# Opening stage of a hybrid diffusion layer on channel-major inputs: token sums by matmul, scalings moved from GpSimd to other engines, late modulation sums formed as columns

## The chip, the cores and the metric

The kernel runs on one core of one Trainium2 chip. Its engines are TensorE (PE in the profile, with its weight loads as PEld), VectorE (DVE), ScalarE (ACT), GpSimd (POOL) and SyncE (SP), whose queue starts all the loads that matter here. The metric is the device time of one execution in microseconds (us). The kernel before took 1308.92 us, the median of 3 runs (1308.15 to 1310.53).

## The reference, cut to what matters

The reference is one layer of a diffusion backbone: 512 latent tokens `x` and 256 context tokens `ctx`, each of 1024 channels, attention and a gated DeltaNet side by side, then a gated MLP. The change touches its first lines, where shift and scale vectors are made from a condition `c`, and both token streams are normalised and modulated with them:

```python
def rms_norm(x, gain=None):
    y = x32 * lax.rsqrt(jnp.mean(x32 * x32, axis=-1, keepdims=True) + NORM_EPS)
...
mod_lat = jax.nn.silu(c) @ w_mod + b_mod          # 6 vectors of 1024: sh1 sc1 g1 sh2 sc2 g2
mod_ctx = jax.nn.silu(c_ctx) @ w_mod + b_mod
hx = modulate(rms_norm(x), sh1, sc1)              # h * (1 + scale) + shift
hc = modulate(rms_norm(ctx), csh1, csc1)
ak_x, av_x, qkv_x, ... = split_cols(hx @ w_in)    # everything else needs hx and hc
```

The first two vectors (`sh1`, `sc1`) are needed at once, by both streams. The other four are needed for the latent stream alone, and late.

## The kernel before

**Precision.** Most products are made from pairs: a 32-bit operand is split into a rounded "hi" (written by ACT as a copy in the type fp32r) and the rest "lo" (a DVE subtraction), and three matmuls (hi·hi, hi·lo, lo·hi) take the place of one. The helper `split` (line 122) does this, `mm3` (126) issues the three matmuls. A matmul on plain 32-bit operands shows up in the profile as two records.

**Opening stage (lines 414 to 583).** Tokens come in with the token on the partition: `xs0` holds the context, `xs1` and `xs2` the latents, 1 MB each. ACT squares each 128x1024 piece and sums it along the row (line 461), GpSimd takes the power -1/2 (`rsqrt`, 172 to 175), and DVE scales the piece in place (465). `x_cols` (502) then turns the scaled tokens channel-major with TensorE transposes, 48 in all, and copies them from PSUM into `stash`, by DVE and ACT in turn.

In the meantime the first 2048 columns of `w_mod` come in as 8 tiles `wm` of 1 MB, in a ring of 3. `gemv(nb)` (469), four of them, multiplies two such tiles by the two condition vectors: the first `FKS[nb]` of the 8 contraction steps as split pairs `wmh`/`wml` (`FKS = '4466'`), the others as plain 32-bit matmuls. `GN = '023'` puts half of the `wml` subtractions of blocks 0, 2 and 3 on GpSimd. `mod_cols(nb)` (489) turns the result into columns of `mod` and `modc`, through a DVE copy `mrow`, 4 small transposes and 4 small DVE additions. Each block `nb` frees two of the 8 channel tiles: `modulate(kp)` (514) scales and shifts those two, for the latents with DVE, for the context with GpSimd (`YV = 2`), and splits the results `hf` into `hxH`/`hxL` and `hcH`/`hcL`. `early_proj(k)` (533) then does the part of channel tile `k` of the first two projections of `w_cm`: 12 matmuls, of 256 and of 512 columns, half each.

**What sets the order.** Between `pinned[0] = True` (541) and 576 every matmul keeps its place in the program, and that place is written out by hand in the string `ORD` (39): `d` is a run of filler matmuls on zeros, `x` is `x_cols`, `g` `gemv`, `m` `mod_cols`, `y` `modulate`, `p` `early_proj`. The loads keep the order of `LORD` (56). Other instructions of DVE, ACT and GpSimd are ordered by a planner, which uses costs of its own and two priorities here: `sooner` (x, g, m, d) goes ahead of `first` (y). Each engine then runs its own list strictly in order.

**The stage behind it (lines 698 to 757).** It begins with the first matmul into `pq` and makes keys, values and queries for six blocks of `w_aq`. Into it `late_mods` (362) is woven, step by step: it computes the other 4096 columns of the modulation (8 groups `q` of 512). ACT, DVE and GpSimd sum 8 scaled tiles `wmd` of the weights into `macc`, 128 partitions by 512. `total(q)` sums over the partitions by a plain matmul with a column of ones as the stationary side (128x1) and `macc` as the moving side (512 columns), giving a row; ACT copies the row to SBUF. `columns(q)`, three steps later, turns the row into 4 columns by 4 transposes, and DVE adds the bias. Both take their PSUM tile from `xbank` (186), which has one buffer (`NX = 1`). What follows (attention, DeltaNet, MLP) is not touched by the change.

Of the kernel before, what the change touches and what calls it, by code (L numbers as in the profile page):

```python
# [6 lines left out]
F32 = mybir.dt.float32  # L7
# [7 lines left out]
P = 128  # L15
# [33 lines left out]
MV, MT, CT = 0, 6, 9  # L49
# [6 lines left out]
LORD = 'x0 x1 x2 w0 w1 w2 w3 h0 h1 w4 w5 w6 w7'  # L56
WB = 3
# [21 lines left out]
def hybrid_layer_body(tc, x, ctxt, xT, consts, cols, rows, w_mod1, w_mod2, w_db, w_aq, w_cm, w_pa, w_pd, w_out,  # L79
# [54 lines left out]
    with es:  # L134
# [227 lines left out]
        def late_mods():  # L362
# [28 lines left out]
            for i in range(9 * KT + CT - 7):  # L391
                for at, fn in ((MT, total), (CT, columns)):
                    q = (i - KT - at) // KT
                    if (i - at) % KT == 0 and 0 <= q < 8:
                        fn(q)
                if i < 8 * KT:
                    part(i // KT, i % KT)
                yield
# [16 lines left out]
        with m1_es:  # L415
            m1 = m1_es.enter_context(tc.tile_pool(name="m1", bufs=1))
            mps = m1_es.enter_context(tc.tile_pool(name="mps", bufs=NB, space=PSUM))
            xs = [m1.tile([P, 2, D], F32, name=f"xs{i}") for i in range(3)]
            wms = []

            def ordered_load(out, in_):
                i = SP.dma_start(out, in_)
                if LPIN:
                    tc.keep_in_program_order(i)

            hw = []
            for op in LORD.split():
                i = int(op[1])
                with sooner():
                    if op[0] == "w":  # L430
                        wms.append(m1.tile([P, 4, 512], F32, name="wm", tag="wm", bufs=WB))
                        ordered_load(wms[i], w_mod1[i // 2, i % 2])
                    elif op[0] == "h":
                        h, part = order[i]
                        raw = ws.tile([P, 1024], F32, name="wraw", tag="wraw", bufs=2)
                        ordered_load(raw, w_cm[8 * part + h])
                    elif i == 0:
                        ordered_load(xs[0], ctxt)
                    else:
                        ordered_load(xs[i], x[:, 2 * i - 2:2 * i, :])  # L440
# [16 lines left out]
            ss = m1.tile([P, 6], F32, name="ss")  # L457
            rs = m1.tile([P, 6], F32, name="rs")
            for i in range(3):
                for t in range(2):  # L460
                    act(hxH[:, 6:8, :].rearrange("p a b -> p (a b)"), xs[i][:, t, :], AF.Square, accum_out=ss[:, 2 * i + t:2 * i + t + 1])
                sl = slice(2 * i, 2 * i + 2)
                rsqrt(rs[:, sl], ss[:, sl], 1.0 / D, EPS)
                for t in range(2):
                    ts(xs[i][:, t, :], xs[i][:, t, :], rs[:, 2 * i + t:2 * i + t + 1], ALU.mult)
            m2 = lambda t, o: t[:, o:o + 16].rearrange("p (s k) -> p s k", s=2)
            wsl = lambda k: slice(k * P, k * P + P)

            def gemv(nb, k0=0, k1=KT):
# [3 lines left out]
                for k in range(k0, k1):  # L473
                    wm, j = wms[2 * nb + k // 4], k % 2
                    if k >= int(FKS[nb]):
                        mm(ps[0:2], cs[:, 2 * k:2 * k + 2], wm[:, k % 4, :], False, k == KT - 1)
                        continue
                    if j == 0:
                        wmh = m1.tile([P, 2, 512], F32R, name="wmh", tag="wmh", bufs=WHB)
                        wml = m1.tile([P, 2, 512], F32R, name="wml", tag="wml", bufs=WHB)  # L480
                        act(wmh, wm[:, k % 4:k % 4 + 2, :])
                        tt(wml, wm[:, k % 4:k % 4 + 2, :], wmh, ALU.subtract, G if k % 4 == 0 and str(nb) in GN else V)
# [16 lines left out]
            sides = ((hxH, hxL, mod, hx_pair), (hcH, hcL, modc, hc_pair))  # L499
            stash = [[pair(F32) for _ in range(KT // 2)] for pair in (hx_pair, hc_pair)]  # L500

            def x_cols(j):
                i, kp = j // 4, j % 4
                dst = stash[1][kp] if i == 0 else stash[0][kp][:, :, 256 * i - 256:256 * i]
                pt = mps.tile([P, 2, 256], F32, name="pt", tag="pt", bufs=NB - PMB - NS)
                for a in range(2):
                    for t in range(2):
                        transpose(pt[:, a, t * P:(t + 1) * P], xs[i][:, t, wsl(2 * kp + a)])
                if j % 2 or j < XV:
                    act(dst, pt)  # L510
                else:
                    V.tensor_copy(dst, pt)

            def modulate(kp):
                for (hh, hl, md, pair), st in zip(sides, stash):
                    n = hh.shape[2]
                    hfs = []
                    for a in range(2):
                        k = 2 * kp + a
                        hf = m1.tile([P, n], F32, name="hf", tag="hf%d" % n, bufs=HB)  # L520
                        if n == NL or YV:
                            ts(hf, st[kp][:, a, :], md[:, 8 + k:9 + k], ALU.mult, md[:, k:k + 1], ALU.add,
                               G if YV == 2 and n < NL else V)
                        else:
                            act(hf, st[kp][:, a, :], AF.Identity, scale=md[:, 8 + k:9 + k], bias=md[:, k:k + 1])
# [20 lines left out]
            def warm(n):  # L546
                pz = mps.tile([P, 512], F32, name="pt", tag="pt", bufs=NB - PMB - NS)
                for i in range(4 * n):
                    mm(pz, wz[:, 0:P], wz)


            def step(what, i):
                if what == "g":
                    with sooner():
                        gemv(i)
                elif what in "ab":
                    with sooner():
                        gemv(i, 0 if what == "a" else 4, 4 if what == "a" else KT)
                elif what == "m":
                    with sooner():  # L560
                        mod_cols(i, mrows[i])
                elif what == "d":
                    with sooner():
                        warm(i)
                elif what == "x":
                    with sooner():
                        x_cols(i)
                elif what == "y":
                    with first():
                        modulate(i)  # L570
                else:
                    early_proj(i)

            for op in ORD.split():
                step(op[0], int(op[1:]))
# [936 lines left out]
def _layout(i):  # L1512
# [5 lines left out]
    a["x"] = f(x.reshape(4, P, D).transpose(1, 0, 2))  # L1518
    a["ctxt"] = f(cx.reshape(2, P, D).transpose(1, 0, 2))
    a["xT"] = f(x.T.reshape(KT, P, NL).transpose(1, 0, 2))  # L1520
# [41 lines left out]
_ORDER = ["x", "ctxt", "xT", "consts", "cols", "rows", "w_mod1", "w_mod2", "w_db", "w_aq", "w_cm", "w_pa", "w_pd",  # L1562
# [21 lines left out]
```

## Time and profile before

| | us |
|---|---|
| median of 3 runs (lowest, highest) | 1308.92 (1308.15, 1310.53) |
| profiled execution, its own time | 1304.85 |
| span of its instructions | 1303.1 |
| opening stage: from the span's start to the first matmul into `pq` | 70.49 |
| stage behind it: to the first matmul of attention scores (`pS`) | 184.48 |
| busy over the span: PE, DVE, ACT, POOL | 1224.8, 846.9, 625.9, 308.9 |

How to read it: the span runs from the first to the last instruction of one profiled execution, and 1.75 us of that execution's time lie around it. An engine counts as busy from the start to the end of each instruction, and matmuls overlap, so a busy PE can still be one that could go faster. A line number such as L108 is that of the helper which issues the instruction (`tt` is 107 to 108, `ts` 110 to 114, `act` 119 to 120, `mm` 131 to 132 with its matmul recorded at L87), so groups are told apart by the names of their tiles: out<-in.

### The profile page before, as it was taken

Reading aid. Unit: us, or ns where it says so; the run is one execution under the profiler, and the core shown is the slowest. Engines: PE = TensorE matmul, PEld = TensorE weight load, DVE = VectorE, ACT = ScalarE, POOL = GpSimd, SP = SyncE. Lnnn points to the kernel's source line nnn. Section 1 sums busy time; section 2 is a strip of 40 time slices with the busy share of each in tenths; the row PEclk is TensorE's granted clock in tenths of the full one; section 3 lists DMA queues with packets and bytes.
Section 4 is the critical chain, followed back from the end, with each engine's and each line's share of the span. In section 5 each row is a group of like instructions: output and inputs, shape, how many; then the busy total and the mean of one; then the engine's idle time right before and its main releaser. Section 6 shows DMA issues by size and latency. Waiting matters only on the chain.

```text
span 1303.1 us, 20844 instructions
## 1 busy us (share of the span) xinstructions
PE 1224.8 (94%) x7835; PEld 1024.0 (79%) x7835; DVE 846.9 (65%) x1625; ACT 625.9 (48%) x1403; POOL 308.9 (24%) x364
## 2 busy tenths in 40 slices
PE   6899999999967999899998999999999999999997
PEld 3487878899856878778787888778988888888886
DVE  5886977777759986675665556555676666653223
ACT  5454656666576665474444443233454444442221
POOL 1753420000133249659546400000000000000000
PEclk9999999999989999999999999999999999999998
DMA  8656731121383342543632654374032323332331
GB/s 318 228 169 200 233 109 65 65 82 57 116 239 104 123 141 93 177 135 106 195 123 97 188 169 147 120 234 155 19 112 97 97 97 97 97 93 89 98 93 66
DMA packets 70790, 170.82 MB, mean 131 GB/s; under 512 B 7872, under 2 KB 18720, under 8 KB 69280
## 3 DMA queue, kind: packets, MB, share of 16 engines
q1 hardware_dynamic: 70688, 169.47, 39.4%
q8 instruction: 62, 1.02, 0.3%
q14 instruction: 40, 0.33, 0.1%
HBM read 144.23 MB, written 25.21 MB: 130 GB/s over the span
## 4 chain that ended last, share of the span: by engine, by line
PE 66%; POOL 11%; DVE 8%; DMA 5%; issue 3%; ACT 3%; SPq 0%; POOLq 0%; DVEq 0%; ACTq 0%
PE mc L87 32%; PE mb L87 17%; POOL R L108 4%; PE pq L87 4%; POOL prod L108 4%; PE pb L87 4%; PE pS L87 3%; PE ab L87 2%; PE ab L91 1%; DMA Gb<-gamdr 1%; DMA M<-gamdr 1%; PE xb L91 1%; DVE wlo L108 1%; PE pk L87 1%; DMA sz<-gdr 1%
## 5 line engine op out<-in xcount | busy, mean ns | idle before, releaser
L108 DVE TENSOR_TENSOR wlo<-wraw,whi 128x1024 fp32r<-128x1024 f32 x152 | 187.5, 1235 | 163.3 <-ACT whi L120 161.1
L120 ACT ACTIVATE whi<-wraw 128x1024 fp32r<-128x1024 f32 x152 | 159.0, 1048 | 207.3 <-PE mc L87 112.0
L87 PE MATMUL mb<-hxH,whi 128*128 128x512 f32 x384 | 163.6, 426 | 3.2 <-DVE R L108 3.0
L87 PE MATMUL mb<-hxL,whi 128*128 128x512 f32 x384 | 153.6, 400 | 0.0
L87 PE MATMUL mb<-hxH,wlo 128*128 128x512 f32 x384 | 153.2, 399 | 0.0
L87 PE MATMUL mc<-h2H,whi 128*128 128x512 f32 (+1 forms) x376 | 142.9, 380 | 0.3 <-ACT whi L120 0.3
L87 PE MATMUL mc<-h2H,wlo 128*128 128x512 f32 (+1 forms) x376 | 142.1, 378 | 0.5 <-DVE wlo L108 0.5
L87 PE MATMUL mc<-h2L,whi 128*128 128x512 f32 (+1 forms) x376 | 140.7, 374 | 0.0
L108 POOL TENSOR_TENSOR rc<-rc,mhalf 128x2 f32<-128x2 f32 x4 | 3.2, 812 | 461.2 <-DVE rc L114 461.2
L87 PEld LDWEIGHTS mb<-hxH,wlo 128*128 128x128 f32 x384 | 73.1, 190 | 18.0
L87 PEld LDWEIGHTS mb<-hxH,whi 128*128 128x128 f32 x384 | 73.9, 192 | 14.8 <-issue 3.2
L87 PEld LDWEIGHTS mc<-h2H,wlo 128*128 128x128 f32 x376 | 70.5, 188 | 15.3 <-DVE wlo L108 1.0
L87 PEld LDWEIGHTS mb<-hxL,whi 128*128 128x128 f32 x384 | 73.7, 192 | 10.1
L87 PEld LDWEIGHTS mc<-h2L,whi 128*128 128x128 f32 x376 | 70.6, 188 | 13.7
L87 PEld LDWEIGHTS mc<-h2H,whi 128*128 128x128 f32 x376 | 70.7, 188 | 12.7 <-ACT whi L120 0.5
L87 PE MATMUL mc<-aH,whi 128*128 128x512 f32 (+1 forms) x198 | 73.4, 371 | 0.6 <-DVE x L117 0.6
L87 PE MATMUL mc<-aH,wlo 128*128 128x512 f32 (+1 forms) x198 | 73.1, 369 | 0.0
L87 PE MATMUL mc<-aL,whi 128*128 128x512 f32 (+1 forms) x198 | 73.1, 369 | 0.0
L117 DVE SCALAR_TENSOR_TENSOR u<-mc,col,u 128x511 f32<-128x511 f32 x88 | 65.4, 747 | 1.4
L108 POOL TENSOR_TENSOR prod<-X,R 128x31 f32<-128x31 f32 (+15 forms) x93 | 53.5, 575 | 22.2 <-DVE X L108 15.3
L108 POOL TENSOR_TENSOR R<-R,prod 128x31 f32<-128x31 f32 (+15 forms) x93 | 57.1, 614 | 6.8
L87 PE MATMUL pq<-whi,hxH 128*128 128x256 f32 x192 | 55.8, 291 | 0.0
(354 smaller groups left out, 3069.8 us busy)
## 6 DMA issues: line engine op xcount, KB each, us to landing
wraw<-in_w_cm_dram SPq DMA_DIRECT2D x48, 512.0 KB, 3.9
wraw<-in_w_up_dram SPq DMA_DIRECT2D x44, 512.0 KB, 3.7
wmd<-in_w_mod_dram SPq DMA_DIRECT2D x64, 256.0 KB, 3.7
wm<-in_w_mod_dram SPq DMA_DIRECT2D x8, 1024.0 KB, 8.9
wraw<-in_w_down_dram SPq DMA_DIRECT2D x16, 512.0 KB, 3.6
wraw<-in_w_aq_dram SPq DMA_DIRECT2D x12, 512.0 KB, 4.9
M<-gamdr SPq DMA_DIRECT2D x64, 64.0 KB, 4.5
wraw<-in_w_pa_dram SPq DMA_DIRECT2D x8, 512.0 KB, 4.0
```

What stands on the lines that cost most here:

```text
L87: i = nc.tensor.matmul(*a, **k)
L91: i = nc.tensor.transpose(*a, **k)
L108: (eng or V).tensor_tensor(out=out, in0=a, in1=b, op=op)
L117: V.scalar_tensor_tensor(out=out, in0=a, scalar=s, in1=b, op0=op0, op1=op1)
L120: A.activation(out, a, f, **kw)
```

## The change

- `x` and `ctx` are loaded channel-major (`xT` as 4 loads of 512 KB into `stash`, `ctxT` as one of 1 MB into `cin`). The 48 transposes, the copies out of PSUM and the scaling of `xs` go.
- `sums(i)`, for i = 0 to 5, takes 128x1024 elements: ACT squares them into `sq` (a ring of 2), DVE adds the two halves, and 4 plain 32-bit matmuls with the squares as the stationary side (128x128) and a 128x128 block of ones as the moving side add up over channels, so that each token's sum stands on its partition. After the last one two DVE operations and one GpSimd power give `rc`, 128x6.
- `spread()` makes diagonal blocks from `rc` (DVE) and multiplies them by ones (plain 32-bit matmuls of 512 and 256 columns), which gives the factor of each token on every partition, in PSUM. `normal(kp)`, four of them, multiplies `stash` by it on DVE.
- The `hf` of `modulate` are made by ACT for both streams. All `wml` are made by DVE (`GN = ''`). `FKS` goes from 4466 to 2466.
- `wm` comes in as 16 tiles of 512 KB in a ring of 7.
- `ORD` changes: 12 filler matmuls in place of 16; `gemv` 0 in two halves (`a0`, `b0`) around `spread`; `p0` and `p1` together behind `m1`; `p2` and `p3` behind `m2`; `p4` to `p7` behind `m3`. `HB`, the ring of `hf`, goes from 2 to 3. `r` and `s` have the priority `sooner`, `n` has `first`.
- In `late_mods` `total` goes; `columns(q)` stands where `total(q)` stood, and makes the 4 columns directly, by 4 plain matmuls with a 128x128 block of `macc` as the stationary side and one column of ones as the moving side.

```diff
-GN = '023'
-FKS = '4466'
-ORD = 'd4 x0 x1 x2 x3 x4 x5 x6 x7 g0 x8 x9 x10 x11 m0 y0 g1 m1 y1 p0 g2 p1 m2 y2 p2 g3 p3 m3 p4 y3 p5 p6 p7'
+GN = ''
+FKS = '2466'
+ORD = 'd3 s0 s1 s2 s3 s4 s5 a0 r0 n0 n1 n2 n3 b0 m0 y0 g1 m1 y1 p0 p1 g2 m2 y2 p2 p3 g3 m3 y3 p4 p5 p6 p7'
-HB = 2
+HB = 3
-LORD = 'x0 x1 x2 w0 w1 w2 w3 h0 h1 w4 w5 w6 w7'
-WB = 3
+LORD = 'c0 x0 x1 x2 x3 w0 w1 w2 w3 h0 h1 w4 w5 w6 w7'
+WB = 7
...
-            def total(q):
-                ps = xbank()[0:1, :, :].rearrange("p a b -> p (a b)")
-                mm(ps, ones[:, 0:1], accs[q][1])
-                act(accs[q][0][0:1, :], ps)
-
             def columns(q):
                 pst = xbank()[:, 0, 0:4]
                 for i in range(4):
-                    T.transpose(pst[:, i:i + 1], accs[q][0][0:1, i * P:(i + 1) * P], ident[0:1, 0:1])
+                    mm(pst[:, i:i + 1], accs[q][1][:, i * P:(i + 1) * P], ones[:, 0:1])
                 tt(mod[:, 16 + 4 * q:20 + 4 * q], pst, col[:, S_BMOD + 16 + 4 * q:S_BMOD + 20 + 4 * q], ALU.add)
...
+            def sums(i):
+                n = (NCX, NL)[i > 1]
+                src = cin[:, 4 * i:4 * i + 4, :] if i < 2 else stash[0][i - 2]
+                sq = m1.tile([P, 1024 // n, n], F32, name="sq", tag="sq", bufs=2)
+                act(sq, src, AF.Square)
+                h = 512 // n
+                tt(sq[:, 0:h], sq[:, 0:h], sq[:, h:2 * h], ALU.add)
...
+                for a in range(h):
+                    for t in range(n // P):
+                        mm(pv[-1][:, t, :], sq[:, a, wsl(t)], ones, i in (0, 2) and a == t == 0,
+                           i in (1, 5) and a == h - 1 and t == n // P - 1)
+                if i == 5:
+                    for o, t in ((4, pv[0][:, 0:2, 0]), (0, pv[1][:, :, 0])):
+                        sl = slice(o, o + t.shape[1])
+                        ts(rc[:, sl], t, 1.0 / D, ALU.mult, EPS, ALU.add)
+                    tt(rc, rc, mhalf[:, 0:6], ALU.pow, G)
+
+            def spread():
+                for s in range(2):
...
+                    tt(dg, ident.unsqueeze(1).to_broadcast([P, n, P]),
+                       rc[:, 4 * s:4 * s + n].unsqueeze(2).to_broadcast([P, n, P]), ALU.mult)
+                    mm(pr[:, 0:n * P], ones, flat(dg))
+                    prs.append(pr[:, 0:n * P])
+
+            def normal(kp):
+                for s in range(2):
+                    tt(stash[s][kp], stash[s][kp], prs[s].unsqueeze(1).to_broadcast([P, 2, prs[s].shape[1]]), ALU.mult)
...
-                        tt(wml, wm[:, k % 4:k % 4 + 2, :], wmh, ALU.subtract, G if k % 4 == 0 and str(nb) in GN else V)
+                        tt(wml, wm, wmh, ALU.subtract, G if k % 4 == 0 and str(nb) in GN else V)
...
-                        if n == NL or YV:
-                            ts(hf, st[kp][:, a, :], md[:, 8 + k:9 + k], ALU.mult, md[:, k:k + 1], ALU.add,
-                               G if YV == 2 and n < NL else V)
-                        else:
-                            act(hf, st[kp][:, a, :], AF.Identity, scale=md[:, 8 + k:9 + k], bias=md[:, k:k + 1])
+                        act(hf, st[kp][:, a, :], AF.Identity, scale=md[:, 8 + k:9 + k], bias=md[:, k:k + 1])
```

More of the change, by code (lines that the diff above doesn't have):

```diff
@@ L48 @@
 NS = 2
-MV, MT, CT = 0, 6, 9
+MV, MT = 0, 6
 MACT, MK, MU = 1, 2.6, 0
@@ L417, in hybrid_layer_body @@
             mps = m1_es.enter_context(tc.tile_pool(name="mps", bufs=NB, space=PSUM))
-            xs = [m1.tile([P, 2, D], F32, name=f"xs{i}") for i in range(3)]
-            wms = []
+            sides = ((hxH, hxL, mod, hx_pair), (hcH, hcL, modc, hc_pair))
+            cin = m1.tile([P, KT, NCX], F32, name="cin")
+            stash = [[hx_pair(F32) for _ in range(KT // 2)], [cin[:, 2 * i:2 * i + 2, :] for i in range(KT // 2)]]
+            wms, hw = [], []
             def ordered_load(out, in_):
[L422 to L426, printed above, removed]
+                tc.keep_in_program_order(SP.dma_start(out, in_))
             for op in LORD.split():
```

97 lines of the change are left out of this document (34 added, 63 removed).

## The prediction

> **What bounds the kernel now.** I first read busy time by stage: the opening from 29.4 to 70.5 us in two stretches, then the stage behind it in two.
>
> ```profile
> core 0: us, PE busy (x) PEld busy (x) DVE busy (x) ACT busy (x) POOL busy (x), PEclk, DMA share, GB/s
> 29.40:49.40 20.00, 16.99 (x67) 7.28 (x65) 17.14 (x28) 11.44 (x17) 13.57 (x7) 0.91 0.87 325
> 49.40:70.50 21.10, 18.65 (x96) 12.55 (x96) 16.32 (x26) 7.76 (x14) 16.04 (x10) 1.00 0.34 113
> 70.50:130.00 59.50, 56.17 (x428) 49.08 (x427) 45.57 (x109) 29.09 (x78) 21.70 (x18) 1.00 0.61 197
> 130.00:184.50 54.50, 51.91 (x401) 45.40 (x400) 52.44 (x151) 33.13 (x102) 23.43 (x16) 1.00 0.61 198
> ```
>
> In the opening no engine is full: DVE has 17.14 of 20.00 us, and GpSimd carries 13.57 and 16.04. Behind it PE is nearly full, and in the second half DVE too. Next, the waits up to 70.5 us, and every instruction on the tiles `wml` and `hf` (shortest/median/longest in ns).
>
> ```profile
> POOL hf L114 <- DVE modc L108: 13.5, 3, 11.6
> ACT hxH L120 <- DVE hf L114: 11.0, 4, 4.3
> ```
> ```profile
> L108 POOL TENSOR_TENSOR wml<-wm,wmh x5: 2391/2476/3367, 17.8 to 51.5; 128x1024 fp32r<-128x1024 f32 x5
> L108 DVE TENSOR_TENSOR wml<-wm,wmh x5: 1209/1214/2630, 20.7 to 50.0; 128x1024 fp32r<-128x1024 f32 x5
> ```
> ```profile
> L114 DVE TENSOR_SCALAR hf<-hxL,mod x8: 534/544/2214, 30.0 to 61.8; 128x512 f32<-128x512 f32 x8
> L120 ACT ACTIVATE hxH<-hf x8: 612/626/635, 30.7 to 62.5; 128x512 fp32r<-128x512 f32 x8
> L114 POOL TENSOR_SCALAR hf<-hcL,modc x8: 553/1566/3114, 31.8 to 64.2; 128x256 f32<-128x256 f32 x8
> L108 DVE TENSOR_TENSOR hxL<-hf,hxH x8: 677/682/721, 33.2 to 63.2; 128x512 fp32r<-128x512 f32 x8
> L120 ACT ACTIVATE hcH<-hf x8: 417/418/421, 35.0 to 64.7; 128x256 fp32r<-128x256 f32 x8
> L108 DVE TENSOR_TENSOR hcL<-hf,hcH x8: 424/426/1507, 35.5 to 66.2; 128x256 fp32r<-128x256 f32 x8
> ```
>
> GpSimd needs 2.48 us for a subtraction that takes DVE 1.21, and DVE's own runs stretch up to 2.63 us (an `hf` from 0.54 to 2.21). So the modulation, GpSimd and ACT waiting for DVE in turn, limits the opening more than the matmuls do.
>
> **The opening, part by part.** I follow PE, whose order is written out, and let the other engines hold it up. The rows for its pace:
>
> ```profile
> 94.73 3.00 PE pq L87 x24
> 97.73 8.30 PE mb L87 x48
> 108.87 0.95 PE xb L87 x2
> 112.86 0.34 PE xb L91 x4
> ```
> ```profile
> 22.80 3.60 PE L87 MATMUL pm<-wm,cs 128*2 128x512 f32 x8
> ```
> ```profile
> 917.97 0.60 PE L87 MATMUL mc<-dg,cst 128*128 128x128 f32 x4
> ```
> ```profile
> 6.85 1.06 ACT L120 ACTIVATE hxH<-xs 128x1024 fp32r<-128x1024 f32 x1 [2.25 <-DMA xs<-in_ctxt_dram]
> ```
>
> 24 matmuls of 256 columns take 3.00 us, 0.125 each. The 8.30 us hold 24 of 256 and 24 of 512, which leaves 0.22 for one of 512. A plain 32-bit one of 512 columns (two records) costs 3.60/4 = 0.90, one of 128 columns 0.60/2 = 0.30. One `early_proj` is 6 x 0.125 + 6 x 0.22 = 2.1.
>
> Sums: the context lands at 6.85 as now. Square 1.06, addition 0.68 (the `hxL` row, same shape), 4 matmuls 1.2: 2.94 us per piece, and with two buffers one piece each 1.5. PE starts at 8.6 and ends at 8.6 + 5 x 1.5 + 1.2 = 17.3, if its clock is full. It may not be:
>
> ```profile
> 8.00:9.00 1.00, 0.00 (x0) 0.00 (x0) 0.00 (x0) 0.97 (x3) 0.00 (x0) 1.00 1.03 434
> 12.00:13.00 1.00, 1.00 (x6) 1.00 (x5) 0.39 (x1) 0.00 (x0) 0.70 (x1) 0.50 1.02 434
> 15.00:16.00 1.00, 0.75 (x5) 0.42 (x4) 0.23 (x1) 0.97 (x3) 0.00 (x0) 1.00 0.99 418
> ```
>
> After some idle microseconds the granted clock was 0.50 at 12, and 1.00 again at 15. The change leaves PE idle for some 3 us ahead of the first sums, so I charge one piece's matmuls twice: +1.2, end at 18.5. The Trainium skill ("TensorE: Matmul & The Clock Gate", "What's actually happening") has the clock halved after an idle window of about 3.4 us and restored after a busy one, which speaks against fewer fillers; by a full window the end would be about an estimated 19.0. The same page ("PE-mode transpose") says that transposes don't count as busy work for this; the trace disagrees, as only transposes ran between 11 and 15, so swapping them for matmuls buys no clock.
>
> Then `a0`: 2 split steps (4 x 0.22) and 2 plain (1.8), 2.7, to 21.2. This hides the reciprocals: the power, two small DVE operations and the diagonals (0.68 + 0.43, as additions of 512 and 256), some 2 us that would all show without `a0`.
>
> ```profile
> 9.46 0.70 POOL L108 TENSOR_TENSOR rs<-rs,mhalf 128x2 f32<-128x2 f32 x1 [9.02 <-DVE rs L114]
> ```
>
>  `spread` 0.9 + 0.45, to 22.5; `b0` 4 x 0.9, to 26.1. For the turn into columns:
>
> ```profile
> L487 DVE COPY mrow<-pm 4x512 f32<-4x512 f32 x4 | 2.7, 674 | 1.6 <-PE pm L87 1.6
> L120 ACT ACTIVATE t<-pc,col 128x256 f32<-128x256 f32 x2 | 0.9, 472 | 3.8 <-PE pc L87 3.8
> L120 ACT ACTIVATE t<-mb,col 128x512 f32<-128x512 f32 x1 | 0.7, 690 | 0.2 <-PE mb L87 0.2
> L108 DVE TENSOR_TENSOR mod<-xb,mod 128x4 f32<-128x4 f32 x4 | 0.7, 163 | 0.1
> ```
>
> `m0`: copy 0.67, transposes 0.34, some 0.4 of hops: 1.4, to 27.5. Now block 1 starts at 29.46:
>
> ```profile
> 29.46 0.39 PE L87 MATMUL pm<-wmh,cs 128*4 128x512 f32 x1
> 70.49 0.28 PE L87 MATMUL pq<-whi,hcH 128*128 128x256 f32 x1
> ```
>
> so some 2 us are won by here. `FKS` costs PE 1.8 - 0.9 = 0.9 in it and saves DVE a `wml`. `g1` (8 x 0.22 + 3.6) and `m1` run to 34.3.
>
> Is `p0` ready by then? DVE is free for this from about 18.9, and must do: 3 `wml` and 2 `wlo` (5 x 1.21), diagonals 1.1, `normal` 4 x (1.21 + 0.68) = 7.6, two `mrow` 1.3, four `mod` additions 0.6, `y0` 2 x 0.68 + 2 x 0.43 = 2.2, together 18.9. Back to back these overlap a little (I take off 6%, as 1.14 against 1.21 in this row), so 17.8, to 36.7.
>
> ```profile
> 91.55 1.14 DVE wlo L108
> ```
>
> DVE is late by 2.4 us, because `normal` is new and all `wml` now lie there. From 36.7: `p0` `p1` 4.2, `g2` 12 x 0.22 + 1.8 = 4.5, `m2` 1.4, `p2` `p3` 4.2, `g3` 4.5, `m3` 1.4, `p4` `p5` 4.2, to 61.1. `y3` starts behind `m3` at 56.9 with 0.6 of additions, then ACT: 2 x 0.69 + 2 x 0.63 + 2 x 0.47 + 2 x 0.42 = 4.4, then an `hcL` 0.43, to 62.4. `p6` and `p7` end at 66.6, against 70.49: -3.9. The ends: with PE alone in charge (2.4 less) and no cold sums (1.2 less) 63.0, -7.5; with more gaps on DVE 71.2, +0.7, below.
>
> The `hf` on ACT (8 x 0.69, 8 x 0.47, 9.3 us) are free up to `y2`: `y1` has 10 us of PE work (`p0` `p1` `g2` `m2`) as cover for 4.4 of ACT and 3 `wmh`; without the cover they would cost 4.4 a block. Loads: SP waits with the eighth `wm` tile until `a0`'s `wml` frees the first, near 18.9; `h0`, `h1`, `w4` to `w7` and the tables queue behind it.
>
> ```profile
> wraw<-in_w_cm_dram SPq DMA_DIRECT2D x2, 512.0 KB, 6.2
> ```
>
> At 6.2 us to landing that tile is there by 25.1, and `g1` needs it near 30, so nothing.
>
> **Late sums.** Now 0.95 + 0.34 = 1.29 us of PE per group, and PE has waited for the row's copy:
>
> ```profile
> 148.43 0.31 PE L91 MATMUL xb<-cst,gam 128*96 128x128 f32 x1 [0.69 <-ACT macc L120]
> 182.27 0.40 PE L91 MATMUL xb<-cst,macc 1*128 1x1 f32 x4 [1.10 <-ACT macc L120]
> ```
> ```profile
> 914.58 0.36 PE L87 MATMUL mc<-cst,acc 128*128 128x1 f32 x2
> 914.80 0.36 PE L87 MATMUL mc<-cst,sq 128*128 128x1 f32 x2
> ```
>
> The last two are the new form (128x128 stationary, one column), one each 0.22: 4 x 0.22 = 0.88. That saves 0.41 x 8 = 3.3, with both waits 5.1. But DVE is busy 52.44 of the last 54.5 us and is what comes late next; if PE merely waits for it, 0.5 is left. I take 3.0, nearer to PE's own rows since PE hardly waited for DVE there.
>
> **Sum.** -3.9 - 3.0 = -6.9. The profiled execution took 1304.85 us, 1.75 of it around the span, so it would take 1298.0; the median of the runs lies 4.1 higher, and 1308.92 - 6.9 = 1302.0.
>
> **Rivals.** (1) *PE alone sets the pace*, DVE keeps up: -7.5 and -5.1, 1296.3. For it: DVE idles between the sums, and its stretched runs end when GpSimd falls silent. Against: the 17.8 us above.
>
> (2) *No difference*: DVE takes the place of GpSimd as the bound. At the 17.14/20.00 = 0.86 that it reaches now between 29.4 and 49.4, 17.8 us need 20.7, so `p0` starts at 39.6 (+2.9). PE then idles 5 us and runs at the half clock for some 3 us, as around 12, which costs 1.7: 71.2, so +0.7, and late sums -1.0: 1308.6.
>
> (3) *Slower*: the `hf` on ACT wait for `mod`, and what the planner puts behind them waits too.
>
> ```profile
> 34.98 0.96 ACT L120 ACTIVATE hcH<-hf 128x256 fp32r<-128x256 f32 x2 [2.14 <-POOL hf L114]
> 35.84 2.94 ACT L120 ACTIVATE wmh<-wm 128x1024 fp32r<-128x1024 f32 x3
> ```
>
> Here three `wmh` stood behind an `hcH` that waited 2.14 us. If the `wmh` of each next block stand behind the eight operations of `y`, a block takes 0.6 + 4.4 + 3.1 + 1.2 (last `wml`) + 2.7 (its matmuls and the plain ones) + 1.4 = 13.4, `g1` 14.2 (one `wmh` less, two plain steps more): 27.5 + 14.2 + 26.8 = 68.5 at `m3`, then `y3` 5.5 and two `p`, 78.2, +7.7; late sums -3.0: 1313.6. It decides once more than two of the three blocks are ordered so. Against: `wmh` has the higher priority, and a ring of 7 brings its data early.
>
> **Numbers.** A run here can tell 0.2%, 2.6 us, from no change. Forecast 0.60, (1) 0.15, (2) 0.15, (3) 0.10. So faster 0.75, same 0.15, slower 0.10. The forecast's own range joins DVE's bounds and the late sums', -3 to -10; the whole range reaches to (1) and half-way into (2), 1296.0 to 1307.0.
>
> **What would show it.** The first `pq` matmul near 66.6; `pS` near 177.6; `p0` at about 36.7, waiting for DVE; DVE without gaps from 19 to 36; GpSimd's busy time down by some 25 us (5 x 2.48 + 8 x 1.57); no DVE subtraction over 2 us before 50. I am wrong if the first `pq` comes later than 70, or if ACT's `wmh` sit behind waiting `hf`; wrong on the late part if the stage from `pq` to `pS` does not get at least 0.5 us shorter.

## The result, and the profile after

The changed kernel takes 1322.17 us, the median of 4 runs (1320.44 to 1324.66), against 1308.54 for the kernel before on the same chip. The ratio is 1.0101 (95% interval 1.0084 to 1.0118): about 1% slower, where 1302.0 was forecast. The profiled execution took 1320.86 us, with a span of 1318.8 (before: 1303.1).

The stages of the kernel after, cut as in the prediction: the opening in two stretches, up to the first matmul into `pq`, then the stage behind it up to `pS`.

```profile
core 0: us, PE busy (x) PEld busy (x) DVE busy (x) ACT busy (x) POOL busy (x), PEclk, DMA share, GB/s
29.40:49.40 20.00, 11.48 (x36) 4.75 (x35) 17.82 (x29) 11.10 (x16) 0.00 (x0) 0.76 0.84 302
49.40:80.27 30.87, 28.18 (x129) 17.92 (x129) 13.92 (x29) 16.65 (x30) 4.98 (x4) 0.93 0.26 85
80.27:140.00 59.73, 54.66 (x410) 50.65 (x409) 42.86 (x100) 25.82 (x69) 23.62 (x18) 0.94 0.60 196
140.00:198.45 58.45, 52.96 (x434) 52.24 (x433) 53.67 (x160) 31.91 (x103) 23.07 (x16) 0.96 0.58 185
```

The first `pq` comes at 80.27 instead of 70.49 (+9.8), and the stage behind it takes 118.2 instead of 114.0 (+4.2). The rest of the span is 1.7 longer. GpSimd is indeed silent from 29.4 to 49.4, and TensorE is not the better for it: 11.48 us busy of 20.00, where it had 16.99. DVE has hardly more to do than before (17.82 against 17.14). The granted clock is below 1.00 in every stretch.

The waits of the opening, and the subtractions `wml`, as asked for in the prediction:

```profile
PE xb L91 <- DVE mrow L510: 9.0, 4, 6.0
ACT hf L120 <- DVE mod L108: 12.5, 3, 7.6
ACT wmh L120 <- PE pm L87: 6.9, 2, 6.2
```
```profile
L108 DVE TENSOR_TENSOR wml<-wm,wmh x9: 1203/1217/1226, 20.9 to 56.9; 128x1024 fp32r<-128x1024 f32 x9
```

No subtraction is stretched any more (1226 ns at most, 2630 before). But a single wait for one row `mrow` took 6.0 us. TensorE's rows show it, together with the sums ahead of it:

```profile
10.41 3.78 PE L87 MATMUL pt<-cst,sq 128*128 128x128 f32 x16 [3.91 <-DVE sq L108]
15.04 3.78 PE L87 MATMUL pt<-cst,sq 128*128 128x128 f32 x16 [0.85 <-DVE sq L108]
...
26.26 3.60 PE L87 MATMUL pm<-wm,cs 128*2 128x512 f32 x8
35.86 0.59 PE L91 MATMUL xb<-cst,mrow 4*128 4x4 f32 x4 [6.00 <-DVE mrow L510]
```

The first block's matmuls end at 29.86, and its row is turned at 35.86. What DVE did in between stands in its own list, in the order in which it ran:

```profile
25.94 4.61 DVE L108 TENSOR_TENSOR hxL<-hxL,pt 128x1024 f32<-128x1024 f32 x4 [1.27 <-PE pt L87]
30.47 1.28 DVE L108 TENSOR_TENSOR cin<-cin,pt 128x512 f32<-128x512 f32 x2
31.66 1.22 DVE L108 TENSOR_TENSOR wml<-wm,wmh 128x1024 fp32r<-128x1024 f32 x1
32.80 1.27 DVE L108 TENSOR_TENSOR cin<-cin,pt 128x512 f32<-128x512 f32 x2
34.00 1.22 DVE L108 TENSOR_TENSOR wml<-wm,wmh 128x1024 fp32r<-128x1024 f32 x1
35.13 0.67 DVE L510 COPY mrow<-pm 4x512 f32<-4x512 f32 x1
```

All eight `normal` passes and two subtractions for the next block run ahead of a copy of 0.67 us for which TensorE stands still. (`hxL<-hxL,pt` and `cin<-cin,pt` are `normal` for latents and context.) The copy has the higher priority; why the planner put it last is not shown. Then TensorE pays twice, through its clock:

```profile
12.00:14.00 2.00, 2.00 (x11) 1.90 (x9) 0.00 (x0) 1.06 (x1) 0.00 (x0) 0.50 1.01 412
14.00:16.00 2.00, 1.15 (x5) 0.96 (x5) 1.44 (x3) 1.06 (x1) 0.00 (x0) 0.50 1.04 414
16.00:18.00 2.00, 2.00 (x12) 2.00 (x11) 0.01 (x1) 0.84 (x1) 0.00 (x0) 0.50 1.02 408
34.00:36.00 2.00, 0.14 (x2) 0.14 (x2) 2.00 (x4) 0.00 (x0) 0.00 (x0) 0.50 0.64 203
36.00:38.00 2.00, 2.00 (x8) 0.82 (x9) 2.00 (x2) 0.14 (x1) 0.00 (x0) 0.50 0.65 229
```

The clock is 0.50 for some 10 us around the sums, and again from 33.1 to 39.9, around the end of the idle time. The Trainium skill ("TensorE: Matmul & The Clock Gate", "HAM oscillation — how this bites in real kernels") warns of idle gaps of more than about 3.4 us between bursts; the gap of 6.00 here agrees. Shorter ones were enough too: the clock was 0.50 again from 46.9 to 50.3 and from 60.7 to 64.1, and the only idle time ahead of the second of these was 1.46 us, in which `m2` waited for its row. At 14 to 16 a stretch that was 58% busy did not bring the clock back.

In the late part the new columns cost about what was forecast (0.95 us a group, against 0.88), except where they wait or the clock is low:

```profile
119.06 0.95 PE L87 MATMUL xb<-cst,macc 128*128 128x1 f32 x8
131.85 1.62 PE L87 MATMUL xb<-cst,macc 128*128 128x1 f32 x8 [2.54 <-DVE beta L114]
...
162.64 0.33 PE L91 MATMUL xb<-cst,gam 128*96 128x128 f32 x1 [3.02 <-DVE mod L108]
```

The transposes of `gam`, next in line for the one bank `xbank`, waited 0.69 us before (for ACT) and wait 3.02 now (for DVE).

### The profile page after: what moved, and what is told of

Read it like the earlier page. It is cut to its first block, busy times and chain, and to the rows that moved or that the text cites. A ratio compares the mean times of both kernels' runs of the same rounds, so it can differ in the third digit from the quotient of the medians.

```text
span 1318.8 us, 20858 instructions
## 1 busy us (share of the span) xinstructions
PE 1233.3 (94%) x7851; PEld 1040.7 (79%) x7851; DVE 834.2 (63%) x1624; ACT 625.6 (47%) x1398; POOL 281.4 (21%) x349
## 4 chain that ended last, share of the span: by engine, by line
PE 67%; POOL 10%; DVE 9%; DMA 6%; ACT 4%; issue 3%; SPq 1%; POOLq 0%; DVEq 0%; ACTq 0%
PE mc L87 32%; PE mb L87 17%; PE pq L87 4%; POOL R L108 4%; POOL prod L108 4%; PE pb L87 3%; PE pS L87 3%; PE ab L87 2%; PE ab L91 1%; DVE wlo L108 1%; DMA Gb<-gamdr 1%; PE pm L87 1%; DMA M<-gamdr 1%; PE xb L91 1%; PE pk L87 1%
## 5 line engine op out<-in xcount | busy, mean ns | idle before, releaser
L108 POOL TENSOR_TENSOR rc<-rc,mhalf 128x2 f32<-128x2 f32 (+1 forms) x5 | 4.6, 915 | 484.0 <-DVE rc L114 484.0
L87 PEld LDWEIGHTS mb<-hxL,whi 128*128 128x128 f32 x384 | 74.7, 194 | 10.2
```

Source lines behind the costliest of these rows:

```text
L87: i = nc.tensor.matmul(*a, **k)
L108: (eng or V).tensor_tensor(out=out, in0=a, in1=b, op=op)
```

## The experiments

My theory after this: the opening lost its time because DVE's and TensorE's lists put work ahead of what the other engine waits for, and the half clock followed; the late sums lost by handing the one bank to DVE in place of ACT. The rivals: DVE simply has too much to do without GpSimd; ACT is the bound; the clock alone is at fault.

The context lands at another time from profile to profile: of the twelve with the changed opening, ACT's first square starts at 6.7 to 7.0 in four, at 7.6 in one, and at 8.5 to 8.9 in seven, and everything behind moves with it. So the opening is compared from the first square to the first `pq`. (Before it took 70.49 - 6.85 = 63.6 us, after 80.27 - 8.57 = 71.7.) This leaves something out: in the five profiles with the opening of before, the square starts at 6.7 to 7.0 each time, so a late landing may itself be a cost of the channel-major loads; no run tests it.

One profiled execution stands behind each of the stage figures, the medians behind the ratios. Each ratio is to the kernel before on the same chip, where that kernel's own median lay between 1307.80 and 1309.17. The clock at the sums also differs from profile to profile. open_only has the opening of after, with the same wait of 6.00 us for the row, but two of its three groups of sums ran faster, and its opening is 1.9 us shorter:

```profile
8.71 3.33 PE L87 MATMUL pt<-cst,sq 128*128 128x128 f32 x16 [2.20 <-DVE sq L108]
12.88 2.18 PE L87 MATMUL pt<-cst,sq 128*128 128x128 f32 x16 [0.85 <-DVE sq L108]
```

Differences of that size in the opening column say little by themselves.

| run | median us | ratio to before, 95% interval | first square to `pq` | `pq` to `pS` |
|---|---|---|---|---|
| after | 1322.17 | 1.0101, 1.0084 to 1.0118 | 71.7 | 118.2 |
| open_only | 1315.80 | 1.0063, 1.0040 to 1.0085 | 69.8 | 115.1 |
| late_only | 1312.78 | 1.0026, 1.0011 to 1.0040 | as before | 115.4 |
| mrow_pin | 1319.85 | 1.0085, 1.0070 to 1.0100 | 68.9 | 118.5 |
| fillers | 1321.35 | 1.0097, 1.0082 to 1.0112 | 68.7 | 120.2 |
| g_first | 1313.34 | 1.0038, 1.0014 to 1.0061 | 66.6 | 116.2 |
| gp_wml | 1315.86 | 1.0049, 1.0031 to 1.0068 | 68.4 | 116.9 |
| hf_back | 1318.08 | 1.0062, 1.0042 to 1.0081 | 67.9 | 116.1 |
| comb | 1314.25 | 1.0057, 1.0034 to 1.0080 | 66.1 | 115.2 |
| comb_n | 1314.92 | 1.0056, 1.0039 to 1.0072 | 67.4 | 115.1 |
| comb_n7 | 1306.65 | 0.9983, 0.9967 to 0.9999 | 60.5 | 116.6 |
| ord_n | 1307.07 | 0.9990, 0.9973 to 1.0008 | 59.7 | 114.1 |
| ord_n7 | 1304.28 | 0.9958, 0.9943 to 0.9974 | 59.8 | 114.4 |
| late_mt9 | 1316.03 | 1.0070, 1.0046 to 1.0094 | as before | 120.9 |
| late_keep | 1309.37 | 1.0012, 0.9998 to 1.0025 | as before | 116.7 |
| late_dead | 1311.66 | 1.0015, 1.0001 to 1.0029 | as before | 118.4 |

**Which part: late_only and open_only.** The first is the kernel before with the late sums of the change, the second the kernel after with the late sums of before.

```diff
# late_only, against before; open_only is the reverse of it, against after
-            def total(q): ...
-                    T.transpose(pst[:, i:i + 1], accs[q][0][0:1, i * P:(i + 1) * P], ident[0:1, 0:1])
+                    mm(pst[:, i:i + 1], accs[q][1][:, i * P:(i + 1) * P], ones[:, 0:1])
```

> The kernel before with only the late modulation sums changed (columns by four matmuls with the block of macc as the stationary side). Theory A: the late sums are a gain on PE (0.79 instead of 1.29 us per group), and the 4 us that the stage behind the opening lost in the changed kernel come from how the opening hands over to it: then the first pq stays at 70.5, the stage to pS takes about 110 to 111.5 us instead of 114.0, and the time falls by 2 to 4 us. Rival B: the quicker PE only runs into DVE and the single xbank buffer, idles there, and its clock is halved after it: then the stage takes 116 to 119 us and the time rises by 2 to 5 us.

> The changed kernel with the late sums put back as they were (row, copy, transposes). Theory A: first pq near 80.3, the stage behind it as long as in the changed kernel (118 us) or longer by the 4 us that PE then needs more, time 1322 to 1326. Rival B (the late sums cost the 4 us themselves): first pq near 80.3, the stage back at 114 us, time about 1318.

Both parts lose by themselves, 0.26% and 0.63%, together 0.89% of the whole's 1.01%. In late_only the loss is seen around `gam`, in TensorE's rows:

```profile
144.85 0.95 PE L87 MATMUL xb<-cst,macc 128*128 128x1 f32 x8
149.32 0.45 PE L91 MATMUL xb<-cst,gam 128*96 128x128 f32 x1 [3.52 <-DVE mod L108]
```

The bank is filled at 145.8, and DVE's addition that empties it starts at 149.12, behind the passes queued ahead of it.

**The first row: mrow_pin.** In the kernel after, the copy `mrow`, the `normal` passes and the `mod` additions keep their program order, and that order puts only `n0` ahead of the first block's row.

```diff
-ORD = '... a0 r0 n0 n1 n2 n3 b0 m0 y0 g1 m1 ...'
+ORD = '... a0 r0 n0 b0 n1 m0 y0 n2 g1 n3 m1 ...'
-                    V.tensor_copy(mrows[nb], ps)
+                    tc.keep_in_program_order(V.tensor_copy(mrows[nb], ps))
```

> The changed kernel with the copies mrow, the additions of mod and the scalings of normal kept in program order on DVE, and n1 behind b0, n2 behind y0, n3 behind g1, so that the first mrow no longer queues behind all eight scalings. Theory C: that queue is what the opening lost most by; the wait of PE for mrow falls from 6.0 us to under 1, block 1 runs at the full clock, the first pq comes at 72 to 75 instead of 80.3, and the time falls by 5 to 8 us against the changed kernel. Rival D: the opening is bound by the total of DVE and ACT work: then the wait only moves to p0 or p2, and the first pq stays within 2 us of 80.3.

TensorE's rows:

```profile
28.81 0.41 PE L91 MATMUL xb<-cst,mrow 4*128 4x4 f32 x4 [0.81 <-DVE mrow L510]
35.45 0.41 PE L91 MATMUL xb<-cst,mrow 4*128 4x4 f32 x4 [0.77 <-DVE mrow L510]
39.26 0.58 PE L87 MATMUL pc<-hcL,whi 128*128 128x256 f32 x1 [2.30 <-DVE hcL L108]
...
54.23 0.50 PE L87 MATMUL pc<-hcH,whi 128*128 128x256 f32 x1 [2.65 <-ACT hcH L120]
```

The wait of 6.00 us is 0.81 now and the second row is turned 8.8 us earlier than after, but most of that is given back: `p0` and `p2`, which stand ahead of `g2` and `g3` on TensorE, wait for operands. `pq` comes 2.7 us earlier and the time is 2.3 lower, but the intervals overlap, and two of the three groups of sums ran at the full clock in this profile, as in open_only. Against open_only the opening is only 1.0 us shorter. The long wait was real, and removing it moved the wait on.

**The clock alone: fillers.** The kernel after with 28 filler matmuls for 12.

```diff
-ORD = 'd3 s0 ...
+ORD = 'd7 s0 ...
```

> The changed kernel with 28 filler matmuls ahead of the sums instead of 12, so that PE is not idle between 6.5 and 10.4. Theory E: the idle time halved the clock for the sums; at the full clock they end at about 19 instead of 21.7, b0 ends near 27 instead of 29.9, but DVE does its scalings first and the first pq moves by only 2 to 3 us. Rival F: the sums are bound by the ring of two squares and by ACT and DVE, and the clock of PE doesn't matter: they end within 0.7 us of 21.7.

The sums ran at the full clock:

```profile
18.18 2.05 PE L87 MATMUL pt<-cst,sq 128*128 128x128 f32 x16 [2.67 <-DVE sq L108]
```

Groups of 16 records had taken 3.78 us in after. The first row still waited 4.97 us, but was turned at 33.43 instead of 35.86, and `pq` came 3.0 us earlier, as theory E had it. The stage behind it was 2.0 us longer, and the time fell by 0.8 us only, within its interval. So the clock at the sums is worth up to 3 us of the opening, no less than mrow_pin's gain, and not the whole loss: this opening is still 5 us longer than that of before.

**TensorE's order: g_first.** mrow_pin with the vector products ahead of the projections whose operands are late.

```diff
-... m1 y1 p0 p1 g2 m2 y2 p2 p3 g3 m3 ...
+... m1 y1 g2 p0 p1 m2 y2 g3 p2 p3 m3 ...
```

> The kernel with the latents' first sums pinned ahead (mrow_pin: 1319.85 us, second modulation at 35.45, first pq at 77.56, waits of 0.72 + 2.30 us at p0 and of 2.65 + 0.79 us at p2), with the third and fourth quarters' vector products put ahead of p0/p1 and p2/p3 on TensorE. From m1 on TensorE has about 30 us of work at the full clock (96 matmuls of a p at 1.05 us for six, two vector products of 4.9), so without waits pq would come at about 66. Order theory (TensorE stands at p0 and p2 in an order in which it could have done the vector product): the four waits of 6.5 us and the half clock behind them go, pq at 69 to 72, time 1312 to 1315. Load theory (VectorE and ScalarE, which now do GpSimd's passes, pace the stage whatever TensorE's order): the wait moves to the vector products (their weight splits are queued on VectorE) or to the next quarter's modulation, pq at 75 to 78, time 1317 to 1320.

6.5 us faster than mrow_pin by the medians, 0.47% by the ratios; 2.2 us of it lie in the opening, and `pq` at 74.22 missed the 69 to 72 of the order theory. TensorE now waits in `g2`, twice, for subtractions. DVE's list, below TensorE's two rows, says why:

```profile
39.80 0.58 PE L87 MATMUL pm<-wml,cs 128*2 128x512 f32 x1 [2.26 <-DVE wml L108]
45.14 0.58 PE L87 MATMUL pm<-wml,cs 128*2 128x512 f32 x1 [3.47 <-DVE wml L108]
```
```profile
40.35 2.33 DVE L490 TENSOR_TENSOR hxL<-hxL,pt 128x1024 f32<-128x1024 f32 x2
42.61 1.27 DVE L490 TENSOR_TENSOR cin<-cin,pt 128x512 f32<-128x512 f32 x2
43.81 0.14 DVE L520 TENSOR_TENSOR mod<-xb,col 128x4 f32<-128x4 f32 x1
43.88 3.47 DVE L108 TENSOR_TENSOR wml<-wm,wmh 128x1024 fp32r<-128x1024 f32 x3
...
50.83 0.14 DVE L520 TENSOR_TENSOR modc<-xb,modc 128x4 f32<-128x4 f32 x1
```

The `normal` passes for the third and fourth pair, which nobody needs before 55 us, take 3.5 us ahead of the second block's additions, which are done at 50.97 although their row was turned at 36.3.

**The load: gp_wml, hf_back and comb.** Each gives work back to where the kernel before has it: five `wml` to GpSimd (the expectations count six, the traces show five); the latents' `hf` to DVE and the context's to GpSimd; and, on g_first, the five `wml` with the old late sums.

```diff
-GN = ''                                   # gp_wml, comb
+GN = '023'
-                        act(hf, ...)      # hf_back
+                        ts(hf, st[kp][:, a, :], ..., V if n == NL else G)
```

> mrow_pin with six of the weight subtractions of the modulation's vector products given back to GpSimd, as the kernel before has them (1.21 us each off VectorE; on GpSimd they took 2.9 us each before and slowed VectorE's own passes to 2.6). Load theory: VectorE, which is busy without a gap from 35 to 54 in mrow_pin, loses 7.3 us of passes, the waits for hcL and for the modulation sums shrink, pq at 72 to 75, time 1314 to 1317. Order theory: p0 still waits for operands that were queued late, pq within 1 us of 77.5, time within 2 us of 1319.9. If the shared contention between the two engines eats the gain, pq is also within 1 us.

> mrow_pin with the modulated inputs hf back where the kernel before has them: the latents' on VectorE (8 passes, 0.55 us undisturbed), the contexts' on GpSimd (1.8 us each there), none on ScalarE (16 passes, 10.3 us off it). Load theory with ScalarE as the bound: the wait for hcH of 2.65 us at p2 goes and p0's operands come as in the kernel before (hcL at 36.3 instead of 39.5), pq at 72 to 75, time 1314 to 1317. Load theory with VectorE as the bound: VectorE gets 4.4 us more and the modulation sums come later still, pq at 78 to 80, time 1320 to 1323. Order theory: within 1 us of 77.5 and 2 us of 1319.9.

> g_first (1313.34 us, pq at 74.22) with six weight subtractions given back to GpSimd and the kernel before's late sums. VectorE theory (VectorE's list from 26 to 54 us sets the opening: in g_first it is busy without a gap from 38 to 54 and TensorE waits 2.26 and 3.47 us for its subtractions): three of the four subtractions of the third quarter that g_first has on VectorE between 43 and 52 are halved in number, pq at 71 to 73; with the late sums of before the stage from pq to pS is 114 to 115 instead of 116.2; time 1307 to 1310. If TensorE's order or the clock is what is left, pq stays at 74 and the time is 1311 to 1312.

Counted from the first square the three gain 0.5, 1.0 and 0.5 us over their base. The medians of gp_wml and hf_back are 4.0 and 1.8 us below that of mrow_pin, but the interval of hf_back overlaps that of mrow_pin. So the load is worth something: the time of gp_wml fell into the range of its load theory, though its `pq` (75.39) missed 72 to 75 and most of the gain isn't in the opening. In the opening neither comes near the 8 us that were lost, and comb, which has the old late sums as well, missed its 1307 to 1310. These runs make DVE's load and ACT's unlikely as the main cause; the next ones decide.

**The order in DVE's list: comb_n, comb_n7, ord_n, ord_n7.** comb_n is comb with `n2` and `n3` behind the second and third blocks' vector products; ord_n is comb_n with all `wml` on DVE, as the change has them; the names with a 7 have 28 fillers.

```diff
-ORD = 'd3 ... m0 y0 n2 g1 n3 m1 y1 g2 p0 p1 m2 y2 g3 p2 p3 m3 ...'
+ORD = 'd3 ... m0 y0 g1 m1 y1 g2 n2 p0 p1 m2 y2 g3 n3 p2 p3 m3 ...'      # comb_n
-GN = '023'
+GN = ''                                                                  # ord_n
```

> comb with the third and fourth latent pairs' normalising passes (1.17 + 0.64 us each on VectorE) put behind the second quarter's modulation sums in VectorE's list instead of ahead of them (in g_first those sums ended at 50.97 with their row ready at 36.3). VectorE theory: the second quarter's hf starts some 10 us earlier, no wait above 1.5 us is left between 36 and 60, pq at 67 to 70, time 1303 to 1307, faster than the kernel before (1309.2). If VectorE's total load counts and not the order in its list, pq is within 1 us of comb's. If the transfers of the weights (DMA share about 1.0 to 38 us) set the time, pq is not below 70.

> comb_n with 28 warming matmuls instead of 12 ahead of the channel sums (granted clock 0.50 from about 10 to 18 us in the kernel after, 1.00 with 28 in the run fillers, sums' end 20.2 instead of 21.9). Clock theory: the sums end 1 to 2 us earlier, the first modulation row and pq as much, time 1 to 2 us below comb_n. Transfer theory (the squares wait for the inputs' arrival, and the first vector product for its weights): pq within 0.5 us and time within 1 us of comb_n.

> comb_n (1314.92 us, pq at 76.03 with waits of 4.13 us for GpSimd's subtraction) with all weight subtractions on VectorE, as the changed kernel has them. Order theory (VectorE can carry GpSimd's six subtractions, 1.21 us each, if none stands ahead of what TensorE waits for): pq at 73 to 76, time 1311 to 1315, not slower than comb_n, since VectorE's own passes are no longer slowed by GpSimd (hcL 2.91 us beside it, 0.74 without). Load theory (the six passes do not fit): pq at 78 to 81, time 1317 to 1320.

> comb_n7 (1306.65 us, pq at 69.40) with all weight subtractions on VectorE. Order theory: pq at 68 to 71, time 1305 to 1309, so the opening without GpSimd's passes is as fast as the kernel before, and what failed in the change was the order of VectorE's and TensorE's lists. Load theory: 7.3 us more on VectorE between 20 and 55 us show as waits for wml and mod, pq at 73 to 77, time 1311 to 1315.

comb_n did not gain: GpSimd was late instead, as TensorE's row, DVE's (with GpSimd at work beside it) and GpSimd's own show.

```profile
56.69 0.59 PE L87 MATMUL pm<-wml,cs 128*2 128x512 f32 x1 [4.13 <-POOL wml L108]
```
```profile
42.71 2.91 DVE L108 TENSOR_TENSOR hcL<-hf,hcH 128x256 fp32r<-128x256 f32 x2
```
```profile
49.29 7.35 POOL L108 TENSOR_TENSOR wml<-wm,wmh 128x1024 fp32r<-128x1024 f32 x1 [3.94 <-ACT wmh L120]
```

The subtraction that TensorE waited for took GpSimd 7.35 us, beside a busy DVE, where the shortest took 2.35. In comb_n7 the planner laid out the two engines otherwise, the longest took 2.99, and that wait is 0.71; so the 6.9 us between the two are not the clock's alone. With all subtractions on DVE both kernels have a short opening: ord_n and ord_n7 take 59.7 and 59.8 us from the first square to `pq`, 3.9 less than the kernel before and 12 less than the kernel after, with the same passes on DVE and no subtraction on GpSimd. The closest comparison is open_only, from which the edit of ord_n differs in the order alone: 10.1 us of opening, and 1.0063 against 0.9990. The load theory had asked for 78 us or later for `pq` in ord_n; it came at 66.44. Its second block's additions, done at 50.97 in g_first, end with this row:

```profile
38.69 0.15 DVE L526 TENSOR_TENSOR modc<-xb,modc 128x4 f32<-128x4 f32 x1
```

The same stages in ord_n7:

```profile
29.40:49.40 20.00, 17.95 (x78) 7.54 (x77) 18.43 (x30) 15.67 (x25) 0.00 (x0) 1.00 0.80 273
49.40:68.30 18.90, 17.10 (x87) 11.99 (x86) 13.08 (x27) 10.39 (x20) 7.66 (x4) 1.00 0.37 115
```

DVE is as full as after (18.43 of 20.00 us), GpSimd as silent, and TensorE has 17.95 where it had 11.48. Behind the sums the clock was at 0.50 for 13.7 us of the opening in after, 6.8 in ord_n and not at all in ord_n7: the order pays twice, by the waits and by the clock that they cost. At 0.9958 of the kernel before, ord_n7 is the fastest of all. Counted from the span's start, `pq` is 4.1 us earlier than before in ord_n and 2.2 in ord_n7. Why the median of ord_n7 is 2.8 below that of ord_n, whose opening is as short, isn't settled; their intervals just touch.

**The late sums: late_mt9, late_keep and late_dead.** All three are the kernel before with its columns made from `macc`, at the step where it has its transposes. late_mt9 has no `total`; late_keep keeps it, though nobody reads its row; late_dead keeps its two matmuls without ACT's copy.

```diff
             def total(q):                      # late_keep, late_dead; not in late_mt9
                 ps = xbank()[0:1, :, :].rearrange("p a b -> p (a b)")
                 mm(ps, ones[:, 0:1], accs[q][1])
-                act(accs[q][0][0:1, :], ps)    # not in late_dead
```

> The kernel before with the late sums as columns alone (late_only: 1312.78 us, 1.0026 of before), with the columns made three steps later, where the kernel before makes its transposes. Place theory (at the earlier step the sums are not ready, so TensorE stands, and the only bank xbank is held until VectorE's addition): the waits for macc, beta and mod come down to the kernel before's or under (macc under 0.5 us, beta under 1.7), time 1305 to 1309. Price theory (the 128-column form itself or the way the later work is laid out by the planner costs): time 1311 to 1314 whatever the step.

> The kernel before with its column sums made twice: its own pass with ones as stationary side (2 matmuls of 512 columns and ScalarE's copy) is kept at its place, its result unread, and the columns come from the accumulators, three steps later, as in late_mt9 (1316.03 us). It differs from late_mt9 by this pass alone, and from before by eight matmuls of one column (0.95 us) for four transposes (0.41). Cover theory (the stage is paced by VectorE, busy 10.00 of 10 from 130 to 170 us in the kernel before; the removed pass only filled TensorE's idle time and kept the granted clock at 1.00): the time comes back to 1308 to 1311 although work is added, and the half clock in the windows of 90 to 150 us goes. Price theory (the one-column form is what costs): 1314 to 1318.

> late_keep (1309.37 us) without ScalarE's copy of the old sums: the two matmuls of 512 columns run at their place into the bank, nobody reads them, and the columns come from the accumulators three steps later. If TensorE's own time there is what counts (it spaces the list and keeps the granted clock), 1308 to 1311, as late_keep. If the copy on ScalarE, which frees the bank at once, is what counts, 1313 to 1317, as late_mt9.

A later step didn't help: 1316.03 us. Work that nobody needs did: with the old pass kept, 1309.37, not to be told from the kernel before, and that with the new columns. So the one-column form costs little here (0.12%, at most 0.25%, though the stage is 2.7 us longer in its profile); the absence of the old pass costs more. late_dead lies in between, and its interval overlaps that of late_keep and not that of late_mt9: TensorE's 1 us per group counts for most of it, ACT's copy for little. late_mt9, then late_keep, in the windows where they differ most:

```profile
130.00:140.00 10.00, 3.95 (x34) 3.72 (x32) 9.96 (x27) 5.41 (x15) 2.90 (x2) 0.83 0.60 193
140.00:150.00 10.00, 7.36 (x46) 7.36 (x47) 4.08 (x17) 2.22 (x9) 3.16 (x2) 0.66 0.32 113
```
```profile
130.00:140.00 10.00, 10.00 (x79) 8.97 (x79) 9.93 (x28) 7.10 (x19) 2.91 (x2) 1.00 0.42 138
140.00:150.00 10.00, 9.32 (x75) 8.22 (x74) 9.71 (x37) 5.08 (x21) 4.32 (x3) 1.00 0.84 270
```

DVE is full from 130 to 140 in both. In late_mt9 TensorE idles meanwhile, waits 8.69 us for a DVE result (`da`), and has 0.66 of its clock in the second window:

```profile
142.64 1.08 PE L87 MATMUL mb<-da,trt 128*128 128x48 f32 x4 [8.69 <-DVE da L112]
```

Two things are mixed in this, and no run here parts them. Without the pass the planner also orders DVE's list otherwise: the chain that leads to `da` is spread over 14 us in late_mt9 and over 8 in the kernel before. And TensorE has less to keep its clock up with: stretches at 0.50 that begin between `pq` and `pS` add up to 10 to 17 us in all eight profiles without the pass, and to no more than 6.8 us in the nine with it. The clock isn't all of it: late_keep has none of that, and its stage is 2.7 us longer than before.

## Why the prediction was wrong, point by point

- **The step that failed first was `m0`, at 27.5.** I let the row go as soon as its matmuls were done, and put DVE's whole lateness (2.4 us) at `p0`. The list had all of `normal` and two `wml` ahead of the row's copy, and it was turned at 35.86. The 17.8 us of DVE work that I counted up to `p0` were about right for the passes named, but the list also held three `wml` of the third block and a third `wlo` ahead of `p0`'s last operand, 4.9 us more. I had a sum of durations for DVE where an order was needed.
- **The clock behind a wait** stood in my sum only at the sums, and there for one piece (1.2); the forecast put nothing for it behind `p0`'s wait. It was at 0.50 from 33.1 to 39.9, 46.9 to 50.3 and 60.7 to 64.1.
- **How the 13.7 us between 66.6 and 80.27 came together**, by TensorE's rows: 3.8 at the end of `b0` (1.7 of it the landing of the context), 5.2 at `m0`, 1.4 in `g1` and `m1`; 1.7 less at `p0`, whose 2.4 I had charged in full; 5.3 from `p0` to the end of `m3`, with waits of 0.70 and 1.05 us at `p0` and 1.46 at `m2` and two stretches at the half clock; 0.3 less behind it.
- **The sums** were to end at 18.5 and ended at 21.9. The half clock held for two groups of 16 records, four pieces of the six. fillers won 1.6 us at this end, and 0.8 in the time.
- **The size of the gain** in the opening was not out of reach: ord_n and ord_n7 gain 3.9 us from the first square on. That this is the number that I forecast is partly chance, since they run in another order than the one that I followed.
- **GpSimd's share.** Right: 308.9 - 281.4 = 27.5 us less, and no stretched subtraction. But taking the work off GpSimd was no gain by itself: every pass had to find a place in DVE's list, and the place was what counted.
- **The late sums**: -3.0 forecast, and +3.9 measured for this part alone (late_only, 0.11% to 0.40%). The price per group was right, the step "if PE merely waits for it, 0.5 is left. I take 3.0" was not. DVE's 52.44 of 54.5 us stood in my own first table and said that TensorE's time in that stage wasn't for sale; I put no loss on the other side. How much of the loss is DVE's order and how much TensorE's clock stays open.
- **Rival (2)**, DVE in GpSimd's place, named the engine that TensorE waited for, but not the cause: ord_n carries the same load. **Rival (3)** has the right sign and not the mechanism: the third block's `wmh` did not stand behind waiting `hf` (the last two ran at 37.86 and 39.56, the first `hf` at 40.53); the fourth block's three did, at 53.43, behind an `hf` that had waited 1.76, so one block was ordered so where the rival needed more than two. ACT also did stand still for 6.2 us ahead of a `wmh`, but for TensorE, which was waiting for the row.
- The rest of the span, +1.7, stays unexplained. From `pS` on nothing is edited, but the planner's layout can differ from kernel to kernel, as it does in comb_n and comb_n7.

## What to carry to other kernels

When work moves to an engine that runs its list in order, a sum of durations is not enough: ask of each short instruction that another engine waits for (here a copy of 0.67 us) what the list has ahead of it, and write that order out by hand if a planner may choose it. Time taken off an engine is a gain only in a stage that it bounds; in the late stage here, which DVE bounds for long stretches, TensorE's freed time became idle time, and idle time went with a lower clock. And when a change loses, try its order before giving it up: the same opening, reordered, with 28 fillers and the late sums of before, beats the kernel before by 0.42% (0.26% to 0.57%); with 12 fillers (ord_n) the two can't be told apart.

## What the runs showed of the hardware that I had not expected

- One load of 1 MB at the start of the program was there for ACT at 6.7 us in some executions and at 8.9 in others, with the same loads ahead of it (the channel-major one; the other form was there at 6.7 to 7.0 in all five profiles).
- Up to 200 us the half clock came in whole pieces of 3.4 us in all seventeen profiles: its stretches, added up from windows of 1 us, last 3.4, 6.8 or 10.2. In the opening of after, what TensorE did in the 3.4 us ahead went with each change: it was busy for 21%, 4%, 26% and 57% of them ahead of the four falls, and for 95%, 100%, 100% and 100% ahead of the four rises, while pieces at 64%, 75% and 20% ended without a rise. One profile doesn't give a threshold, but idle time needn't be in one gap.
- Eight plain 32-bit matmuls of 128 columns (16 records) took 2.05 us at the full clock in fillers and 3.78 at 0.50 in the kernel after: the granted clock is felt nearly in full (1.84 times) even by matmuls as small as these.
- Beside GpSimd at work two DVE subtractions of 128x256 took 2.91 us in comb_n, against 0.74 in mrow_pin. It goes both ways: GpSimd's subtraction of 7.35 us above ran beside DVE's passes, the shortest took 2.35. The Trainium skill ("GPSIMD Engine Reference", "Key points") says that the two engines share SBUF interfaces and that DVE instructions with two SBUF inputs contend; the runs agree.
